# A second level of Strassen's scheme for one product in four pairs of column groups, in a fused encoder block on one core

## The chip, the core and the metric

The kernel runs on one core of a Trainium2 chip. It has TensorE (PE, matrix products; weight loads are shown as PEld), VectorE (DVE), ScalarE (ACT), GpSimd (POOL) and SyncE (SP, whose queue issues the transfers). The metric is the device time of one execution in microseconds (us); lower is better. Work is in float32 split into two float16 parts (a high part and what is left, the low part), so one product of two matrices is three matrix products: high × high, high × low, low × high (`PASSES`).

## The reference

One encoder layer over 1024 tokens of width 1024:

```python
u = rms_norm(x, norm1_g)
q, k, v, cb, cc, ch, ga, gb = jnp.split(u @ w_in, split_pts, axis=-1)
q, k = rms_norm(q, q_norm_g), rms_norm(k, k_norm_g)        # 8 heads of 64
y_a = neighbourhood_attention(q, k, v, rpb) @ w_attn_branch
y_b = short_gated_conv(cb, cc, ch, conv_w) @ w_conv_branch
merged = jax.nn.sigmoid(ga) * y_a + jax.nn.sigmoid(gb) * y_b
x = x + merged @ w_o
h = rms_norm(x, norm2_g) @ w_mlp_in                        # 1024 -> 4096
x = x + jnp.square(jax.nn.relu(h)) @ w_mlp_out             # 4096 -> 1024
```

## The kernel before

The stages follow each other on TensorE: V, Q and K with attention and convolution, the gates (eight blocks `n` of channels), the product with `w_o`, the first MLP product (`w_mlp_in`), the second (`w_mlp_out`). The change lies in the gates, in the first MLP product and in the way from it to the second.

**First MLP product.** The 4096 columns are done in 16 groups `q` of 256 columns. Each group is one level of Strassen's scheme in Winograd's form: the weights of the group and the activations are cut into 2 × 2 quarters, and `seven` does seven products (numbers 1 to 7) of the quarters' sums in place of eight. A product is a `unit` of twelve matmuls of 512 tokens (four slices of the inner dimension times three passes) into one of eight PSUM banks, which `anybank` hands out in turn. Groups 0 and 1 run in two halves of 256 tokens, groups 2 to 15 whole (`quad`). VectorE and ScalarE put the seven results together in the tile `as` (`z[0]` to `z[6]`): ScalarE copies product 1 into `z[4]`, VectorE adds product 6 (`z[5]`), and so on (`post6`, `post5`, `post7`, `post3`). Then `h_done` applies ReLU and Square on ScalarE, GpSimd adds the sums that the second product will need, and SyncE stores the tile in `HS`.

Ahead of it, `prep1` and `sums1` get the weights of a group ready: SyncE loads two raw tiles of 512 KB, ScalarE multiplies by `norm2_g` (`rows_scaled`), GpSimd adds the four sums of quarters (`tsum`), ScalarE takes Squares of the raw tiles for a scale (`forms_sum`), a matmul with a column of ones adds these over the partitions (L201, `all_sum`), VectorE makes the scale from it in six short instructions (`scale_of`), and ScalarE and VectorE write the high and the low parts (`forms_split`, L1184, L1188). The parts `w16_1` of consecutive groups lie in three buffers in turn (`TAGS`), so that group `q`'s may be written when group `q - 3` is done (`gate`).

**Second MLP product.** 28 steps `ops[16]` to `ops[43]`, each a product of high and low parts made from `h` (loaded back from `HS`) and from sums of the `w_mlp_out` tiles (`raw`, `w2x`). `prep2` gets the scale of a quarter of these weights (L1751, L1754, L1139, the ones matmul, L204) and then the parts: ScalarE the high parts (L1786, L1791), VectorE the low parts (L1788, L1797). A step waits in the program for the buffers of three steps before.

**What sets the order.** The order is made when the program is built: each `unit` on TensorE advances generators in the background (`tick` for `bg`, which gets weights ready; `step` for `fg`, which finishes results) by so many steps, and each step appends its instructions to its engine's queue. The engines then run their queues in that order. SyncE's queue is one as well: a load that waits for a free raw tile holds back all behind it. `load_upto` appends loads as raw tiles are said to be done.

Of the kernel before, what the change touches and what calls it, by code (L numbers as in the profile page):

```python
# [10 lines left out]
F32 = mybir.dt.float32  # L11
# [41 lines left out]
def encoder_block(ctx: ExitStack, tc: tile.TileContext, x, weights, cols, gqk, rel, masks, out):  # L53
# [24 lines left out]

    sc = base.tile([128, 540], F32, name="sc")
    sci = sc.bitcast(I32)  # L80
    area = {"keep": [0, 0, 172], "prep": [172, 172, 268], "tmp": [268, 268, 540]}

# [14 lines left out]
    def at(c, i, n=1):  # L97
        return slice(c.start + i, c.start + i + n)
# [79 lines left out]

    late, units, forced, side = [], [0], [False], [False]
    work = [0]  # L180
# [5 lines left out]
    def built(*chs):  # L186
# [5 lines left out]
        forced[0] = False  # L192
    ones, turn = base.tile([128, 132], BF16, name="ones"), [0]
    V.memset(ones, 1.0)
# [11 lines left out]

    def unit(mms, post=None, steps=0, ticks=0):

        for ps, l, r, a, b in mms:
            T.matmul(ps, l, r, start=a, stop=b)  # L210
# [126 lines left out]
    consts = keep(28)  # L337
    g1, g2, gm2 = at(consts, 0, 8), at(consts, 20, 8), keep()
    rows = {"A": lambda j: rowsA, "B": lambda j: rowsB, "O": lambda j: rowsM}
    chunks, offset = {}, 0  # L340
    for (kind, j), pieces in plan():
        ch = chunks[kind, j] = Chunk(kind, [(nk, sum(n for _, n in cs)) for _, _, nk, cs in pieces],
                                     {"A": "wa", "B": "wb"}.get(kind, "ws"), rows.get(kind, lambda j: g1)(j),
                                     j if kind == "V" else None, 9 if kind in "VQKCGS" else 0)
        ch.first = len(loads)
        for p, (k, w) in enumerate(ch.widths):
            ch.offs.append(offset)
            if kind != "X" and (kind, j) != ("1", 0) and (kind, j, p) != ("1", 1, 1):
                loads.append((ch, p))
            offset += 128 * k * w  # L350
    cG, cS = chunks["G", 0], {n: chunks["S", n] for n in range(1, 8)}
    cV, cConv, cA, cB, cO, c1, c2, c2x = ([chunks[k, j] for j in range(n)] for k, n in
# [888 lines left out]
    def gate_units(n, tail=None):  # L1241
# [32 lines left out]
        return sg  # L1274

    def branch_units(n, post):
        j, cc = n // 2, (n % 2) * 128
        for g, act, ch in ((0, actA, cA[j]), (1, actB, cB[j])):
            built(ch)
            for half in range(2):  # L1280
                ps = anybank()
                unit(ch_mms(ps, act, half, ch, 4, 256, cc),
                     lambda ps=ps, g=g, half=half, ch=ch: post(g, half, ps, sc[:, ch.inv]), 2, 4)

    for n in range(8):
# [5 lines left out]
        if n < 7:  # L1291
            sg = gate_units(n)
            if n in (1, 3, 5):
                push(cA[n // 2 + 1], cB[n // 2 + 1])
# [147 lines left out]
    def sums1(q):  # L1442

        ch = c1[q]
        if q == 2:
            yield from rows_scaled(ch, g2)
        if q == 0:
            tsum[0] = U2[1][:, 2].rearrange("p s k t -> p (s k t)").bitcast(F32).rearrange("p (i c) -> p i c", i=4)
        elif q % 2 == 0:
            t = wsp.tile([128, 2, 4, 512], F32, name="tsum", tag="ws")  # L1450
            for i in range(2):
                tsum[q + i] = t[:, i]
        if q != 2:
            yield from rows_scaled(ch, g2)
        yield from forms_sum(ch, tsum[q], 3 if q else 0)

    def prep1(q):

        ch = c1[q]
        s, ch.inv = yield from scale_of(ch.sum, 9, 1)  # L1460
        yield from gate(q)
        pool, tag = TAGS[q % 3]
        P = P1[q] = pool.tile([128, 7 if q else 8, 2, 512], F16, name="w16_1", tag=tag)
        yield from forms_split(ch, tsum[q], s, P)
        ready.add(q)
        if 1 < q < 15:
            yield from sums1(q + 1)

# [94 lines left out]

    bg.extend([first1(), prep_m()])
    side[0] = True
# [48 lines left out]
    def last_pair():  # L1614
# [24 lines left out]
    def h_done(q, c0=0, c1=512, wait1=0, wait2=0):  # L1639
# [26 lines left out]
    def quad(q, c0=0, c1=512):  # L1666
# [24 lines left out]
        def post3(ps):  # L1691
# [8 lines left out]
            2: lambda ps: V.tensor_tensor(z[0], ps[2], z[4], op=OP.add),  # L1700
            7: post7, 3: post3}, 2 if c1 == 512 else 3, 5, (1, 2, 5, 4, 6, 7, 3) if c0 else (1, 6, 5, 4, 2, 7, 3))

    def whole(q):
        quad(q)
        pe_done[0] = q + 1

    quad(0, 0, 256)
# [7 lines left out]
    held[0] = 0  # L1715
    for q in range(2, 14):
        whole(q)


# [16 lines left out]
    def prep2(s):  # L1736
# [26 lines left out]
        if s == 0:  # L1763
# [201 lines left out]
```

## Time and profile before

| | us |
|---|---|
| three runs | 1199.51, 1201.03, 1201.32 |
| median | 1201.03 |
| the profiled execution | 1199.51 |
| its span on the core | 1197.7 |
| TensorE busy | 1188.3 (99%) |
| VectorE busy | 939.3 (78%) |
| ScalarE busy | 753.0 (63%) |
| GpSimd busy | 432.9 (36%) |

The granted clock of TensorE is 1.00 in the whole run. In the span, the gates run from about 298 to 530 us, `w_o` to about 612, the first MLP product to 903.7 (groups 0 and 1 in halves to 649.5, then 18.15 us for each group; group 14 starts at 867.40 and group 15 at 885.53), and the second from there to 1191, in steps of 10.36 us. A row of a timeline gives the start, the length, the engine, the line, the instruction with what it writes and reads, and in brackets the idle time before it with what ended that.

### The profile page before, as it was taken

To read this page: it belongs to the slowest core of one execution; us is meant where nothing else is said; L and a number is where in the kernel's file an instruction comes from. 1 tells how busy PE (TensorE), PEld (TensorE's weight loads), DVE (VectorE), ACT (ScalarE), POOL (GpSimd) and SP (SyncE) were. 2 spreads that over 40 slices of the span, in tenths; PEclk is the share of its full clock that TensorE was granted. 3 is DMA by queue.
4 is the path that set the end of the run, shared out by engine and by line. 5 is a ranking of instruction groups with operands and counts; after the bars stand their busy time and mean duration, and the time that the engine had idled before them with its cause. 6 is when DMAs were issued, how large, how long until landed. Compare 5 with 4: busy or idle time off the path is not lost.

```text
span 1197.7 us, 16871 instructions
## 1 busy us (share of the span) xinstructions
PE 1188.3 (99%) x6206; PEld 573.6 (48%) x6206; DVE 939.3 (78%) x1708; ACT 753.0 (63%) x1169; POOL 432.9 (36%) x292
## 2 busy tenths in 40 slices
PE   8999999999999999999999999999999999999998
PEld 6444445555444444444467444444444444444444
DVE  6799898898478786878888745645649999999997
ACT  7866578776554554336779768778576743746440
POOL 2640012222320312001014466565577471554662
PEclk9999999999999999999999999999999999999999
DMA  9949557666452121233386545535465926335302
GB/s 288 220 158 205 114 128 138 116 141 138 104 130 68 38 71 36 71 139 142 74 161 197 177 149 177 170 127 187 159 237 202 376 80 233 112 140 194 106 36 106
DMA packets 177250, 174.91 MB, mean 146 GB/s; under 512 B 137744, under 2 KB 138256, under 8 KB 173072
## 3 DMA queue, kind: packets, MB, share of 16 engines
q1 hardware_dynamic: 177168, 173.84, 49.6%
q8 instruction: 48, 0.79, 0.3%
q14 instruction: 34, 0.28, 0.1%
HBM read 102.51 MB, written 37.75 MB: 117 GB/s over the span
## 4 chain that ended last, share of the span: by engine, by line
PE 79%; DVE 13%; ACT 5%; issue 2%; DMA 0%; POOL 0%; DVEq 0%; ACTq 0%
PE ps_d L210 27%; PE ps_s L210 24%; PE ps_o L210 17%; PE ps_d L1060 8%; DVE w_s L1184 2%; PE ps_s L980 1%; PE ps_o L1037 1%; DVE s L498 1%; DVE sg L1300 1%; ACT w_ws L266 1%; DVE w_ws L297 1%; DVE q L764 1%; DVE qs L751 1%; ACT sq L439 1%; ACT w_ws L306 1%
## 5 line engine op out<-in xcount | busy, mean ns | idle before, releaser
L210 PEld LDWEIGHTS <-ops 128*128 128x128 f16 x1356 | 132.5, 98 | 157.3
L210 PEld LDWEIGHTS <-w 128*128 128x128 f16 x1368 | 132.8, 98 | 139.5
L1060 PE MATMUL ps_d<-uT,w_ws 128*128 128x512 f16 x528 | 123.7, 379 | 0.0
L210 PE MATMUL ps_d<-ops 128*128 128x512 f16 (+1 forms) x528 | 118.3, 374 | 0.0
L1786 ACT ACTIVATE ops<-hf,sc 128x2048 f16<-128x2048 f32 x26 | 52.0, 2000 | 97.7 <-PE ps_o L210 35.2
L210 PE MATMUL ps_s<-ops 128*128 128x512 f16 x492 | 112.9, 379 | 0.0
L1173 POOL TENSOR_TENSOR tsum<-raw 128x512 f32<-128x512 f32 x28 | 46.2, 1665 | 148.9 <-ACT raw L1159 148.7
L1366 POOL TENSOR_TENSOR as<-as 128x512 f32<-128x512 f32 x56 | 77.5, 1385 | 38.4 <-ACT as L1646 35.1
L210 PEld LDWEIGHTS <-w_s 128*128 128x128 f16 x588 | 56.8, 98 | 69.6 <-DVE w_s L1184 2.1
L210 PEld LDWEIGHTS <-uT 128*128 128x128 f16 x528 | 51.4, 98 | 62.1 <-DMA uT<-u 0.2
L210 PE MATMUL ps_d<-u2x,w 128*128 128x512 f16 (+1 forms) x360 | 80.0, 372 | 0.0
L1788 DVE SCALAR_TENSOR_TENSOR ops<-hf,sc,ops 128x2048 f16<-128x2048 f32 x26 | 74.0, 2846 | 4.6 <-ACT ops L1786 4.6
L1060 PEld LDWEIGHTS <-w_ws 128*128 128x128 f16 x528 | 51.3, 98 | 54.1
L210 PE MATMUL ps_o<-ops 128*128 128x512 f16 x336 | 77.1, 379 | 0.0
L210 PE MATMUL ps_o<-u2T,w 128*128 128x512 f16 (+1 forms) x324 | 71.7, 371 | 0.0
L1159 ACT ACTIVATE raw<-raw,sc 128x256 f32<-128x256 f32 x172 | 71.0, 494 | 0.1
L1173 POOL TENSOR_TENSOR gsum<-raw 128x512 f32<-128x512 f32 x14 | 19.0, 1379 | 132.9 <-ACT raw L1159 59.9
L1188 ACT ACTIVATE w<-raw,sc 128x512 f16<-128x512 f32 (+1 forms) x28 | 24.6, 927 | 54.1 <-DVE sc L432 54.1
L1679 DVE TENSOR_TENSOR as<-ps_d,as 128x512 f32<-128x512 f32 (+1 forms) x14 | 9.4, 672 | 55.8 <-ACT as L1698 53.4
L210 PE MATMUL ps_s<-u2T,w 128*128 128x512 f16 (+1 forms) x252 | 52.7, 359 | 0.0
L1003 ACT ACTIVATE sz<-sz,sc 128x384 f32<-128x384 f32 (+1 forms) x64 | 37.3, 582 | 23.9 <-DVE sc L994 16.6
L306 ACT ACTIVATE w_ws<-raw,sc 128x512 f16<-128x512 f32 (+2 forms) x72 | 40.6, 637 | 17.6 <-DVE sc L279 17.6
(374 smaller groups left out, 2621.5 us busy)
## 6 DMA issues: line engine op xcount, KB each, us to landing
raw<-in_weights SPq DMA_DIRECT2D x88, 512.0 KB, 5.3
hs<-as SPq DMA_DIRECT2D x16, 1792.0 KB, 8.8
hf<-hs SPq DMA_DIRECT2D x26, 1024.0 KB, 7.1
w2x<-in_weights SPq DMA_DIRECT2D x16, 512.0 KB, 8.5
raw<-in_weights SPq DMA_DIRECT2D x16, 384.0 KB, 3.8
xt<-in_x SPq DMA_DIRECT2D x8, 512.0 KB, 8.2
gs<-s SPq DMA_DIRECT2D x4, 1024.0 KB, 3.9
x<-in_x SPq DMA_DIRECT2D x8, 512.0 KB, 9.8
```

The source lines that it names most:

```text
L210: T.matmul(ps, l, r, start=a, stop=b)
L266: A.activation(self.parts[:, 1, :k * w].bitcast(BF16), self.raw[p][:, :k * w], AF.Square, accum_out=sc[:, at(rm, p)])
L306: A.activation(self.parts[:, 0, f + o:f + o + m], self.raw[p][:, o:o + m], AF.Copy, scale=sc[:, c:c + 1])
L1003: A.activation(z, z, AF.Exp, scale=-1.0, bias=sc[:, d["mx"]], accum_out=sc[:, d["sm"]])
L1060: T.matmul(ps, l, r, start=a, stop=b)
L1159: A.activation(v, v, AF.Copy, scale=sc[:, at(g, 4 * i + k)])
L1173: G.tensor_tensor(t[:, o], a, b, op=OP.add)
L1184: V.scalar_tensor_tensor(o(1), w, sc[:, s], o(0), op0=OP.mult, op1=OP.subtract)
L1188: A.activation(o(0), w, AF.Copy, scale=sc[:, s])
L1366: sub.tensor_tensor(z[o], z[a], z[b], op=op)
L1786: A.activation(P[:, 1, 0], hf, AF.Copy, scale=sc[:, Rs])
L1788: V.scalar_tensor_tensor(P[:, 1, 1], hf, sc[:, Rs], P[:, 1, 0], op0=OP.mult, op1=OP.subtract)
```

## The change

1. *Second level.* For the pairs of groups (6, 7), (8, 9), (10, 11) and (12, 13), product 1 of both groups of a pair (24 matmuls of 512 tokens) is done as one: the left quarter of both groups, side by side, is cut in 2 × 2 again, and seven products of six matmuls of 256 tokens each give the two results (`slices`). They are summed in three PSUM banks, in three units of 18, 12 and 12 matmuls (`THREE`) with one ordinary product between two of them. ScalarE and VectorE read the banks between the units (`p0`, `p1`, `p2`). The sums of quarters of the activations are made once (`quarters`, in groups 2 and 3), those of the weights for each pair (`deep1`).
2. *Norms early.* The Squares that give the scales of groups 2 to 15 are taken in the gates (`norms1`): the weights are loaded there once more, 28 loads of 512 KB, into three rooms that turn free, and `scales1` makes all scales with one matmul of ones of seven columns.
3. *Buffers and order.* The parts `w16_1` lie in two buffers ("V" and "B"), since the parts of the slices take the third, and are written when group `q - 2` is done. Each background generator prepares a pair (`prep_pair`). The store of a group's result comes four steps later in the program (`wait(4)`), groups 3 to 13 advance the background by two ticks a product, and the matmul of ones of the second MLP product's first scale stands one unit later (`scale_of(sums, 0, 4)`).

The core of the diff:

```diff
-    def unit(mms, post=None, steps=0, ticks=0):
+    def unit(mms, post=None, steps=0, ticks=0, free=False):
         for ps, l, r, a, b in mms:
-            T.matmul(ps, l, r, start=a, stop=b)
+            T.matmul(ps, l, r, start=a, stop=b, skip_group_check=free)
+        for g in list(hooks):
+            if not advance(g):
+                hooks.remove(g)
...
+    def norms1(t, first):
+        for _ in range(first):
+            yield
+        for q in range(2, 16):
+            for i in range(2):
+                if (2 * q + i) % 3 == first:
+                    SP.dma_start(t, bass.AP(tensor=weights.tensor, ...))
+                    for _ in range(4):
+                        yield
+                    A.activation(t, t, AF.Square, accum_out=sc[:, at(sum1, 2 * (q - 2) + i)])
+                    yield
...
     def prep1(q):
-        pool, tag = TAGS[q % 3]
-        P = P1[q] = pool.tile([128, 7 if q else 8, 2, 512], F16, name="w16_1", tag=tag)
+        P = P1[q] = base2.tile([128, 8, 2, 512], F16, name="w16_1", tag="B")
...
+    def main1(q):
...
+        while pe_done[0] < q - 1:
+            yield
+        m = int(deep)
+        pool, tag = ((base, "V"), (base2, "B"))[q % 2]
+        P = pool.tile([128, 7 - m, 2, 512], F16, name="w16_1", tag=tag)
...
+        yield from parts([...], at(s1, q // 2 - 1), then)
+        ready.add(q)
...
+    def deep1(q):
+        x, y = c1[q].r[0], c1[q + 1].r[0]
+        d = sub["t"][:, 1, 0:2].rearrange("p a (h c) -> p (a h) c", h=2)
+        b11, b21, b12, b22 = x[:, 0, :256], x[:, 0, 256:], y[:, 0, :256], y[:, 0, 256:]
+        for o, a, b in ((0, b11, b12), (1, b12, b22), (2, d[:, 0], b22), (3, d[:, 2], b21)):
+            V.tensor_tensor(d[:, o], a, b, op=OP.add)
...
-        bg.append(sums1(2))
-        bg.extend(prep1(q) for q in range(2, 16))
+        sub["t"] = wsp.tile([128, 2, 4, 512], F32, name="tsum", tag="ws")
+        bg.append(prep_pair(2))
...
+        yield from wait(4 if q > 1 else 0)
         SP.dma_start(HS[q // 4][:, :, q % 4], f)
...
+        def p0():
+            A.activation(y, b("a"), AF.Copy)
+            add(zb[:, lo], b("b"), y)
+        def p1():
+            add(zb[:, hi], b("b"), y)
+            less(zb[:, hi], b("c"), zb[:, hi])
+        def p2():
+            A.activation(za[:, lo], b("a"), AF.Copy)
+            add(za[:, hi], b("b"), y)
+            less(zb[:, lo], b("c"), zb[:, lo])
+            ends()
...
+        first = slices(q, 0, z[4], zp, sub["y"], ends)
+        advance(first)
+        need(q)
+        main(q, ps, 5, None)
+        advance(first)
+        main(q, ps, 6, None)
+        advance(first)
+        for i, post in ((2, p2), (4, None), (7, p7), (3, p3)):
+            main(q, ps, i, post, ticks)
...
-    for q in range(2, 14):
+    bg.extend(prep_pair(q) for q in range(4, 16, 2))
+    for q in range(2, 6):
         whole(q)
+    need("quarters")
+    for q in range(6, 14, 2):
+        pair(q)
...
-        sw, inv = yield from scale_of(sums, 0)
+        sw, inv = yield from scale_of(sums, 0, 4)
```

**VectorE, at the end of group 14 and in group 15.** `as_8334` (before) and `as_8364` (after) are group 15's result tile; `h0` and `raw` feed the first low parts, of `ops[16]` (`ops_8263`, `ops_8307`). Before (L1692 is the last post of group 14, L204 to L433 make the scale, L1679 is group 15's first post, L1788 and L1797 write low parts):

```order
L1692 TENSOR_TENSOR as_8207<-ps_d_8318,as_8207 128x512
L204 TENSOR_SCALAR sc_71<-ps_o_8352 128x1
L426 TENSOR_SCALAR sc_71<-sc_71 128x1
L428 TENSOR_SCALAR sc_71<-sc_71 128x1
L430 TENSOR_SCALAR sc_71<-sc_71 128x1
L432 TENSOR_SCALAR sc_71<-sc_71 128x1
L433 TENSOR_SCALAR sc_71<-sc_71 128x1
L1679 TENSOR_TENSOR as_8334<-ps_d_8355,as_8334 128x512
L102 TENSOR_TENSOR sc_71<-sc_71 128x1
L1788 SCALAR_TENSOR_TENSOR ops_8263<-h0_8223,sc_71,ops_8263 128x2048
L1797 SCALAR_TENSOR_TENSOR ops_8263<-raw_7891,sc_71,ops_8263 128x1024
L1797 SCALAR_TENSOR_TENSOR ops_8263<-raw_8039,sc_71,ops_8263 128x1024
```

In the changed kernel L1829 is the last post of group 14, L1816 group 15's first, L204 to L442 make the scale, L2036 and L2045 write low parts:

```order
L1829 TENSOR_TENSOR as_8224<-ps_o_8348,as_8224 128x512
L1816 TENSOR_TENSOR as_8364<-ps_s_8383,as_8364 128x512
L204 TENSOR_SCALAR sc_71<-ps_o_8398 128x1
L435 TENSOR_SCALAR sc_71<-sc_71 128x1
L437 TENSOR_SCALAR sc_71<-sc_71 128x1
L439 TENSOR_SCALAR sc_71<-sc_71 128x1
L441 TENSOR_SCALAR sc_71<-sc_71 128x1
L442 TENSOR_SCALAR sc_71<-sc_71 128x1
L1821 TENSOR_TENSOR as_8364<-ps_d_8401,as_8364 128x512
L102 TENSOR_TENSOR sc_71<-sc_71 128x1
L2036 SCALAR_TENSOR_TENSOR ops_8307<-h0_8269,sc_71,ops_8307 128x2048
L2045 SCALAR_TENSOR_TENSOR ops_8307<-raw_7978,sc_71,ops_8307 128x1024
```

Group 15's first post now stands ahead of the six scale rows, and its second (L1821) ahead of the product of the scales (L102); before, the second came behind the low parts of `ops[16]`.

**SyncE, around the start of group 14.** `hs3` is the store of a result tile (group 12's first, group 13's later), `raw` and `w2x` are loads of weights, `h0` and `ops` loads of stored results. Before:

```order
L1657 DMA hs3_5334<-as_7928 896x1x512
L234 DMA raw_8183<-in_weights 128x1024
L234 DMA raw_8185<-in_weights 128x1024
L234 DMA w2x_8224<-in_weights 128x1024 x4
L1824 DMA h0_8223<-hs0_5331 128x2048
L1657 DMA hs3_5334<-as_8077 896x1x512
L1767 DMA ops_8350<-hs0_5331 128x2048
```

In the changed kernel:

```order
L1794 DMA hs3_5391<-as_7931 896x1x512
L237 DMA raw_8246<-in_weights 128x1024
L237 DMA raw_8248<-in_weights 128x1024
L237 DMA w2x_8270<-in_weights 128x1024 x4
L2072 DMA h0_8269<-hs0_5388 128x2048
L1794 DMA hs3_5391<-as_8106 896x1x512
L2015 DMA ops_8380<-hs0_5388 128x2048
```

The order of the rows is the same; the two raw loads wait for other tiles, those of group 15's weights, whose parts are now written after group 13 is done.

**ScalarE, in one group before and around one slice unit now.** Before, the scaling of raw tiles (L1159), two Squares for the norm (L1168), Relu and Square of the group before (L1644, L1646), the copy of product 1 (L1698), then high parts (L1188):

```order
L1159 ACTIVATE raw_7458<-raw_7458,sc_71 128x2x128 x4
L1159 ACTIVATE raw_7600<-raw_7600,sc_71 128x2x128 x4
L1168 ACTIVATE tsum_7624,sc_71<-raw_7458 128x1024
L1168 ACTIVATE tsum_7624,sc_71<-raw_7600 128x1024
L1644 ACTIVATE as_7639<-as_7639 128x2048
L1646 ACTIVATE as_7639,sc_71<-as_7639,sc_71 128x2048
L1698 ACTIVATE as_7783<-ps_o_7784 128x512
L1188 ACTIVATE w16_1_7884<-raw_7458,sc_71 128x512
L1188 ACTIVATE w16_1_7884<-raw_7600,sc_71 128x2x512
L1188 ACTIVATE w16_1_7884<-tsum_7624,sc_71 128x2x512 x2
L1159 ACTIVATE raw_7602<-raw_7602,sc_71 128x2x128 x4
L1159 ACTIVATE raw_7745<-raw_7745,sc_71 128x2x128 x4
```

In the changed kernel L1511 scales raw tiles, L1866 is the copy in `p0` and L1874 that in `p2` (both read the bank `ps_o_7932`), L1780 and L1782 are Relu and Square, L1197 writes high parts:

```order
L1197 ACTIVATE w16_1_7838<-raw_7680,sc_71 128x2x512
L1197 ACTIVATE w16_1_7838<-tsum_6097,sc_71 128x2x512 x2
L1511 ACTIVATE raw_7682<-raw_7682,sc_71 128x2x128 x4
L1866 ACTIVATE zt4_7042<-ps_o_7932 128x256
L1780 ACTIVATE as_7817<-as_7817 128x2048
L1197 ACTIVATE w16_1_7970<-raw_7682,sc_71 128x2x512
L1782 ACTIVATE as_7817,sc_71<-as_7817,sc_71 128x2048
L1197 ACTIVATE w16_1_7970<-tsum_6097,sc_71 128x2x512 x2
L1874 ACTIVATE as_7931<-ps_o_7932 128x256
L1511 ACTIVATE raw_7684<-raw_7684,sc_71 128x2x128 x4
L1511 ACTIVATE raw_7856<-raw_7856,sc_71 128x2x128 x4
L1780 ACTIVATE as_7931<-as_7931 128x2048
```

The two Squares for the norm are gone, and the copies after the slice units stand each in a place of its own between the other rows.

More of the change, by code (lines that the diff above doesn't have):

```diff
@@ L177, in flush @@
         forced[0] = False
-    late, units, forced, side = [], [0], [False], [False]
+    late, units, forced, side, hooks = [], [0], [False], [False], []
     work = [0]
@@ new lines, in quarters, with pace @@
+    def quarters():
+        def pace():
+            yield from apart(units[0], 1)
+        sub["a"] = wsp.tile([128, 4, 2, 2, 256], F16, name="a16_d", tag="ws")
+        f = base.tile([128, 7, 512], F32, name="quarter", tag="K")
+        u = u2T[:, 0]
+        for t in range(2):
+            hi, lo = (u[:, i, :, 256 * t:256 * t + 256] for i in range(2))
+            V.tensor_tensor(f[:, 2 * t:2 * t + 2].rearrange("p h (k c) -> p (h k) c", k=2), hi, lo, op=OP.add)
+            yield from pace()
+        yield from sums(f, V)
+        for a, b, v in ((0, 1, f[:, 2:3]), (1, 4, f[:, 4:7])):
+            hi, lo = (sub["a"][:, a:b, i].rearrange("p f k c -> p f (k c)") for i in range(2))
+            A.activation(hi, v, AF.Copy)
+            yield from pace()
+            V.tensor_tensor(lo, v, hi, op=OP.subtract)
+            yield from pace()
+        ready.add("quarters")
```

183 lines of the change are left out of this document (162 added, 21 removed).

## The prediction

> **What bounds the kernel now.** I read the page first. Its busy line and the line of the chain that ended last, by engine:
>
> ```profile
> PE 1188.3 (99%) x6206; PEld 573.6 (48%) x6206; DVE 939.3 (78%) x1708; ACT 753.0 (63%) x1169; POOL 432.9 (36%) x292
> ...
> PE 79%; DVE 13%; ACT 5%; issue 2%; DMA 0%; POOL 0%; DVEq 0%; ACTq 0%
> ```
>
> TensorE is busy for 1188.3 of 1197.7 us. The chain's 13% of VectorE only says whose result TensorE took up last. Whether TensorE stands still is seen in its waits (line, what released it, us in total, times, longest):
>
> ```profile
> PE ps_o L565 <- DMA xt<-in_x: 4.6, 1, 4.6
> PE ps_s L980 <- DVE sc L994: 0.5, 1, 0.5
> PE ps_s L210 <- DVE w_s L1184: 0.3, 1, 0.3
> PE ps_d L210 <- DVE w_s L1184: 0.2, 1, 0.2
> ```
>
> That is the first load of x and three waits of half a microsecond or less. So a shorter matmul stream shortens the run one for one, while every other engine may take more work until it makes TensorE wait. Next I read TensorE's timeline in the first MLP product (start, length, instruction, count):
>
> ```profile
> 631.18 1.47 PE L210 MATMUL ps_d<-u2T,w 128*128 128x256 f16 x12
> 632.49 1.47 PE L210 MATMUL ps_s<-u2T,w 128*128 128x256 f16 x12
> ...
> 649.54 2.75 PE L210 MATMUL ps_o<-u2T,w 128*128 128x512 f16 x12
> 652.13 2.75 PE L210 MATMUL ps_d<-u2x,w 128*128 128x512 f16 x12
> ...
> 659.90 0.17 PE L201 MATMUL ps_s<-ones 128*128 128x1 bf16 x1
> 659.93 1.24 PE L210 MATMUL ps_o<-u2T,w 128*128 128x512 f16 x5
> ```
>
> Starts give the stream: twelve matmuls of 256 columns take 632.49 − 631.18 = 1.31 us (109.2 ns each), twelve of 512 take 2.59 us (215.8 ns each), and a one-column matmul of L201 pushes the next by 659.93 − 659.90 = 0.03 us. Last, the other engines' load in two stretches, gates and MLP (span, then length, busy us and count for PE, weight loads, DVE, ACT, POOL; clock, DMA share, GB/s):
>
> ```profile
> 380.00:400.00 20.00, 19.88 (x93) 8.89 (x92) 14.79 (x26) 11.53 (x19) 5.46 (x4) 1.00 0.18 54
> 700.00:750.00 50.00, 50.00 (x235) 22.65 (x234) 27.56 (x50) 38.31 (x58) 30.85 (x23) 1.00 0.50 167
> ```
>
> ScalarE is busy for 11.53 of 20 us in the gates and 38.31 of 50 in the MLP, VectorE 14.79 of 20 and 27.56 of 50. There is room, if the new work falls into the gaps.
>
> **What the change takes from TensorE.** In four pairs, product one of both groups is 2 × 12 matmuls of 512, 24 × 215.8 ns = 5.18 us, and becomes seven slices of six matmuls of 256, 42 × 109.2 ns = 4.59 us. That is 0.59 us a pair, 2.37 us for four. Fourteen one-column matmuls become one: 13 × 0.03 = 0.39 us. Sum: −2.76 us. It counts in full, since nothing else holds TensorE there.
>
> A rule of the Trainium skill speaks against this. "TensorE: Matmul & The Clock Gate", section Back-to-back issue gap, calls N/2.4 + 2.5 ns the gap of an isolated matmul, and gives a sustained spacing of about 81 ns for 128 columns and 131 ns for 512. An estimate on a line between these is 98 ns for 256, by which a pair would lose 42 × 98 − 24 × 131 = 0.97 us, the change 3.9. The rows above, with a weight load for every matmul, don't agree: 215.8 ns and 109.2 ns are what that page gives for the isolated one.
>
> **Norms in the gates.** 28 loads of 512 KB and 28 Squares over 1024 columns come in. The price of a Square is L1168's (gate stage, busy, mean ns):
>
> ```profile
> L1168 ACT ACTIVATE gsum<-raw 128x1024 f32<-128x1024 f32 x14 | 14.8, 1054 | 0.3
> ```
>
> With its read of the accumulator, some 0.2 us, 28 × 1.25 = 35 us of ScalarE over about 190 us that have 8.5 us in 20 free. SP is handed 28 more issues; each waits for the Square that last read its room, and raw loads queue behind. But a load has four TensorE units (10.4 us) ahead of its Square, and at 54 GB/s, a DMA share of 0.18, it has the engines nearly for itself. At most two or three Squares in a row (3.8 us) stand ahead of the splits of the next gate's weights. I take nothing, with 0 to 2 us as its bounds: the low end because TensorE had no wait to lose there, the high end if half of such a burst hits once. In exchange MLP groups 2 to 15 lose 28 Squares and their VectorE scalars: no TensorE time.
>
> **Support for the slices.** Per pair four deep sums and seven 256-wide posts on VectorE, the weight parts of the slices, two 256-wide copies on ScalarE. Prices of the kinds (busy, mean ns):
>
> ```profile
> L1184 DVE SCALAR_TENSOR_TENSOR w<-raw,sc,w 128x1024 f16<-128x1024 f32 x12 | 15.3, 1279 | 0.3 <-ACT w L1188 0.3
> ...
> L1366 DVE TENSOR_TENSOR as<-as 128x256 f32<-128x256 f32 x8 | 3.4, 423 | 0.2
> ```
>
> Eleven × 0.42 = 4.6 us and about 3 us of low parts, less the posts and low parts of two products of 512 which go: some 4 us per pair of 36 us, where VectorE has 16 us free (27.56 of 50). The once-only quarter sums (24 × 256 columns, under 24 × 0.42 = 10 us) push the posts of group 2 back. Weights are ready groups ahead. Nothing, unless slices wait on ScalarE (second rival).
>
> **The way into the second MLP product.** Two buffers for split weights in place of three put the splits of group 15 behind the end of group 13; raw loads freed by them stand ahead of the w2x loads in SP's queue. I count from the first matmul of group 14, t = 0. ops[16] is the second MLP product's first:
>
> ```profile
> 867.40 2.75 PE L210 MATMUL ps_o<-u2T,w 128*128 128x512 f16 x12
> ...
> 903.69 2.75 PE L210 MATMUL ps_s<-ops 128*128 128x512 f16 x12
> ```
>
> ops[16] starts at t = 36.3, ops[17] 4 × 2.59 later at 46.65. What leads there now: SP's issues and the landing of w2x (median us),
>
> ```profile
> 863.80 1.62 SPq L234 DMA_DIRECT2D raw<-in_weights  x2
> 865.48 2.85 SPq L234 DMA_DIRECT2D w2x<-in_weights  x4
> 868.42 0.42 SPq L1824 DMA_DIRECT2D h<-hs  x1
> ```
>
> ```profile
> w2x<-in_weights SPq DMA_DIRECT2D x4, 512.0 KB, 9.2
> ```
>
> then ScalarE (squares L1751, L1754; Relu, Square and z copy of group 14/15; high parts of ops[16]),
>
> ```profile
> 874.34 1.14 ACT L1751 ACTIVATE ops<-raw,sc 128x1024 bf16<-128x1024 f32 x1
> ...
> 879.42 2.00 ACT L1754 ACTIVATE ops<-w2x,sc 128x2048 bf16<-128x2048 f32 x1
> ...
> 881.55 2.00 ACT L1754 ACTIVATE ops<-w2x,sc 128x2048 bf16<-128x2048 f32 x1
> ...
> 887.17 1.91 ACT L1644 ACTIVATE as<-as 128x2048 f32<-128x2048 f32 x1 [3.53 <-DVE as L1692]
> 889.12 2.00 ACT L1646 ACTIVATE as<-as,sc 128x2048 f32<-128x2048 f32 x1
> ...
> 891.12 0.58 ACT L1698 ACTIVATE as<-ps_s 128x512 f32<-128x512 f32 x1
> 891.60 1.99 ACT L1786 ACTIVATE ops<-h,sc 128x2048 f16<-128x2048 f32 x1
> ```
>
> and VectorE:
>
> ```profile
> 883.67 0.16 DVE L1139 TENSOR_REDUCE sc<-sc 128x1 f32<-128x6 f32 x1 [7.61 <-ACT ops L1754]
> ...
> 888.36 0.16 DVE L204 TENSOR_SCALAR sc<-ps_o 128x1 f32<-128x1 f32 x1 [1.22 <-PE ps_o L201]
> ...
> 889.18 0.14 DVE L433 TENSOR_SCALAR sc<-sc 128x1 int32<-128x1 int32 x1
> 891.73 0.69 DVE L1679 TENSOR_TENSOR as<-ps_d,as 128x512 f32<-128x512 f32 x1 [2.40 <-ACT as L1698]
> ...
> 893.62 2.44 DVE L1788 SCALAR_TENSOR_TENSOR ops<-h,sc,ops 128x2048 f16<-128x2048 f32 x1 [1.04 <-ACT ops L1786]
> 895.99 4.50 DVE L1797 SCALAR_TENSOR_TENSOR ops<-raw,sc,ops 128x1024 f16<-128x1024 f32 x2
> ...
> 901.01 3.84 DVE L1788 SCALAR_TENSOR_TENSOR ops<-ops,sc 128x2048 f16<-128x2048 f32 x1
> ...
> 907.89 5.89 DVE L1797 SCALAR_TENSOR_TENSOR ops<-h,sc,ops 128x1024 f16<-128x1024 f32 x2
> 913.71 2.34 DVE L1788 SCALAR_TENSOR_TENSOR ops<-hf,sc,ops 128x2048 f16<-128x2048 f32 x1
> ```
>
> Before: w2x issued at −1.9, its squares end at 16.2, the sum of the norms (L1139) stands at 16.3, the scale is there at 21.9 (889.18 + 0.14), low parts start at 26.2 and ops[17] is ready at 46.4 (907.89 + 5.89). The second half of its first product starts 1.3 us after 46.65 and takes its first low part one matmul later, 48.15: 1.8 us to spare.
>
> After: the last post of group 13 ends at 0.9. ScalarE then has Relu 1.9, a high part of 512 (0.7, from the 1024 below), Square 2.0 and a high part of 1024 ahead; a low part on VectorE frees the raw tile:
>
> ```profile
> L1188 ACT ACTIVATE w<-raw,sc 128x1024 f16<-128x1024 f32 x11 | 12.5, 1133 | 0.0
> ```
>
> That makes 0.9 + 1.9 + 0.7 + 2.0 + 1.1 + 1.3 (the 1279 ns above) = 7.9. The raw load goes, and 0.8 later (two took 1.62) w2x, from 8.7 to 10.8 for the last: 10.6 us later than now. ScalarE, at 6.6 after that high part, has two more (2.3), a z copy (0.6) and the four L1751 squares (874.34 to 879.42, 5.1) before it needs w2x at 14.6, and would end at 18.8 (4.2 for L1754) if the loads were there; with 9.2 us of landing the last is there at 20.0, and the squares end at 22.2. I take 20.4, by the middle. So the norms' sum comes 4.1 later.
>
> The five posts of group 14 behind it on VectorE end at 23.9 (883.67 to 887.17 is 3.5 us); Relu, Square and the z copy of group 15 follow (887.17 to 891.73: 4.56), and the order now has the post on that copy (z5) ahead of the six scale rows, where before the scale went first. So z5 at 28.5, scale at 29.1 + 0.96 = 30.1, high part 1.99, low parts from 32.1: 5.9 later than 26.2. The other post (0.6 us, 900.41 to 901.01) now lies under the high part, so ops[17] is ready at 46.4 + 5.9 − 0.6 = 51.7. With 0.1 us for the signal TensorE has waited 51.8 − 48.15 = 3.65, say **3.7 us**, of it about 1 at ops[16]. With the ends 18.8 and 22.2 it is 2.1 and 5.5. Later products are covered: at 913.71 VectorE was to wait 2.48 us for ScalarE before ops[18], and this idle time goes first.
>
> **Sum.** The profiled execution took 1199.51 us, 1.81 more than its span. 1199.51 − 2.76 + 3.7 = 1200.45. It is the fastest of three runs (1199.51, 1201.03, 1201.32), 1.52 under the median; on the median's footing 1202.0. A measurement can tell 0.2% from no change, 2.4 us: from 1198.6 to 1203.4 is "the same". The forecast's own range is 1200.4 to 1203.8.
>
> **Rivals.**
> - *Clean gain.* The w2x loads land soon and the copy of group 15 slips ahead, or TensorE needs the low parts later than I think; then only −2.76 is left: 1201.03 − 2.76 = 1198.3. For it: the margin of 1.8 us takes part of the delay, and the chain has eight links, each of which I may have too late. Against: each link is in the order of the program. 0.24.
> - *Slices wait (slower).* The second slice unit adds into the banks of the first, so ScalarE's copy and VectorE's add of it must be done within the one product between them, 2.59 us; copy, add and signals are about 1.0, so 1.6 is to spare. If ScalarE stands in a Relu and a Square (1.9 + 2.0 = 3.9 us) as the slice ends, TensorE waits up to 2.3 us, say 1.25, once per pair: 4 × 1.25 = 5.0 us, without or with the 3.7: 1203.3 to 1207.0. It decides from a copy that starts 1.6 us after its slice. Against: the copy stands ahead of the Relu of the group before. 0.20.
> - *Matmul pace (slower).* If matmuls of 256 with three banks open take over 5.18 us / 42 = 123 ns, product one gains nothing; halfway between 109.2 and 215.8, at 162.5 ns, a pair loses 1.65 us: 1201.03 + 6.6 − 0.39 + 3.7 = 1210.9. Against: the 109.2, measured with a weight load for every matmul. 0.03. By the figures of the Trainium skill's page on TensorE (above) alone, the time would be 1201.03 + 3.9 = 1204.9.
> - *A longer wait on the way in.* The forecast's upper end, over 5.1 us: 1203.4 to 1203.8. 0.10.
>
> **Numbers.** Forecast without change 0.43. Faster 0.24, the same 0.43, slower 0.20 + 0.03 + 0.10 = 0.33. The range goes from the clean gain, 1198.3 less 0.5 for spread of runs, to the slices' 1207.0 less 0.5, since its upper end needs both waits: 1197.8 to 1206.5; left out is the matmul pace and the ends of the others.
>
> **What would show it.** Slices: twelve 256-wide matmuls in 1.31 us, three units of 18, 12 and 12. Gates: no TensorE wait over 0.5 us. Group 14 to ops[17]: w2x issued 8 to 9 us after the group's start, L1139's row 20 us after, TensorE idle for about 1 us at ops[16] and 2.7 at ops[17], released by VectorE's low parts (L1797). Wrong if TensorE doesn't wait there, or waits inside the pairs.

## The result and the profile after

The changed kernel takes 1204.39 us (median of 9 runs, 1203.29 to 1205.79) against 1200.11 us for the kernel before (9 runs, 1199.07 to 1201.38): the ratio is 1.0034, interval 1.0024 to 1.0045, so 4.3 us slower. The time lies in the range given, but not where the forecast put it (the same); it is on the side of the slower rivals. The profiled execution took 1205.79 us, the slowest of the nine, with a span of 1204.0. Its busy line and the line of the chain:

```profile
PE 1186.2 (99%) x6265; PEld 579.7 (48%) x6265; DVE 975.0 (81%) x1654; ACT 754.7 (63%) x1175; POOL 455.3 (38%) x292
...
PE 61%; DVE 23%; ACT 8%; issue 5%; DMA 2%; SPq 0%; DVEq 0%; POOL 0%; ACTq 0%
```

TensorE has 2.1 us less to do and yet the span is 6.3 us longer; in the chain VectorE's share went from 13% to 23%. The waits of TensorE (line, releaser, total us, times, longest) say where:

```profile
PE ps_o L574 <- DMA xt<-in_x: 4.5, 1, 4.5
PE ps_s L210 <- DVE ops L2045: 2.6, 2, 1.8
PE ps_s L210 <- DVE w_s L1193: 1.1, 1, 1.1
PE ps_d L210 <- DVE w L1193: 1.1, 1, 1.1
PE ps_d L210 <- DVE as L1824: 0.9, 1, 0.9
PE ps_d L546 <- DVE ones L609: 0.7, 1, 0.7
PE ps_o L210 <- DVE x L2144: 0.7, 1, 0.7
PE ps_d L210 <- DVE ops L2045: 0.7, 1, 0.7
PE ps_s L989 <- DVE sc L1003: 0.5, 1, 0.5
PE ps_d L210 <- DVE w_s L1193: 0.2, 1, 0.2
```

Three lines stood there before: the first load, L989's 0.5 and the 0.2 of w_s. New are 3.3 us at the operands of the second MLP product (L2045), 1.1 us at group 4's weights (L1193 w), 0.9 us at a bank (as L1824), 0.7 us near the end (x L2144); the gates' wait went from 0.3 to 1.1 us, and one of 0.7 us in the first 10 us changes from profile to profile (0 to 1.8). The slices run as fast as forecast: in TensorE's timeline six matmuls start every 0.655 us, 109 ns each.

```profile
724.22 0.82 PE L210 MATMUL ps_d<-u2T,w_d 128*128 128x256 f16 x6
724.88 0.82 PE L210 MATMUL ps_s<-a_d,w_d 128*128 128x256 f16 x6
725.53 0.82 PE L210 MATMUL ps_o<-a_d,w_d 128*128 128x256 f16 x6
```

What is lost is seen when TensorE's starts in the changed kernel are set against those before, place by place:

| place | before, us | after, us | after − before |
|---|---|---|---|
| first attention product | 147.46 | 147.47 | 0.01 |
| `w_o` | 529.86 | 530.79 | 0.93 |
| group 2 | 649.54 | 650.45 | 0.91 |
| ops[16] | 903.69 | 904.29 | 0.60 |
| last unit | 1191.25 | 1196.43 | 5.18 |

A listed wait costs 0.16 us more than it lists, since a matmul is shown for 379 ns and starts every 216. With that, gates 0.85; groups 2 to 15: −2.76 + 1.08 + 0.89 + 2 × 0.16 = −0.47 (the table has −0.31); second MLP product: 3.25 + 0.69 + 4 × 0.16 = 4.58 (the table has 4.58). The sum is 5.0 of 5.2 us. The other 1.1 of the 6.3 us of span lie behind TensorE's work: from the last unit's start to the landing of the last store both kernels take 5.5 us, and then the program's closing semaphore instructions take 0.91 us before and 2.05 after. With one profile of the kernel before, it is not shown whether that belongs to the change.

The way into the second MLP product, after: TensorE (start of group 14, which is t = 0, and of ops[16]), SyncE, ScalarE, VectorE.

```profile
868.00 2.75 PE L210 MATMUL ps_s<-u2T,w 128*128 128x512 f16 x12
...
904.29 1.67 PE L210 MATMUL ps_d<-ops 128*128 128x512 f16 x7
```

```profile
872.31 4.26 SPq L237 DMA_DIRECT2D raw<-in_weights  x2
876.63 1.94 SPq L237 DMA_DIRECT2D w2x<-in_weights  x4
```

```profile
884.16 2.00 ACT L2002 ACTIVATE ops<-w2x,sc 128x2048 bf16<-128x2048 f32 x1 [2.18 <-DMA w2x<-in_weights]
...
887.49 2.00 ACT L2002 ACTIVATE ops<-w2x,sc 128x2048 bf16<-128x2048 f32 x1 [1.23 <-DMA w2x<-in_weights]
...
897.53 1.99 ACT L2034 ACTIVATE ops<-h,sc 128x2048 f16<-128x2048 f32 x1
```

```profile
889.61 0.16 DVE L1148 TENSOR_REDUCE sc<-sc 128x1 f32<-128x6 f32 x1 [7.93 <-ACT ops L2002]
...
897.66 0.69 DVE L1816 TENSOR_TENSOR as<-ps_s,as 128x512 f32<-128x512 f32 x1 [4.58 <-ACT as L1835]
898.27 0.15 DVE L204 TENSOR_SCALAR sc<-ps_o 128x1 f32<-128x1 f32 x1
...
899.81 2.35 DVE L2036 SCALAR_TENSOR_TENSOR ops<-h,sc,ops 128x2048 f16<-128x2048 f32 x1
...
913.97 5.87 DVE L2045 SCALAR_TENSOR_TENSOR ops<-h,sc,ops 128x1024 f16<-128x1024 f32 x2
```

w2x is issued at t = 8.6 (forecast 8.7), ScalarE's squares wait 2.18 and 1.23 us for it, the norms' sum stands at 21.6 (20.4), group 15's first post at 29.7 (28.5), the low parts begin at 31.8 (32.1), and ops[17] is ready at 51.8 (51.7).

### The profile page after: what moved, and what is told of

It is laid out like the page before. It is cut to its first block, busy times and chain, and to the rows that moved or that the text cites. A ratio compares the mean times of both kernels' runs of the same rounds, so it can differ in the third digit from the quotient of the medians.

```text
span 1204.0 us, 16986 instructions
## 1 busy us (share of the span) xinstructions
PE 1186.2 (99%) x6265; PEld 579.7 (48%) x6265; DVE 975.0 (81%) x1654; ACT 754.7 (63%) x1175; POOL 455.3 (38%) x292
## 4 chain that ended last, share of the span: by engine, by line
PE 61%; DVE 23%; ACT 8%; issue 5%; DMA 2%; SPq 0%; DVEq 0%; POOL 0%; ACTq 0%
PE ps_s L210 19%; PE ps_d L210 18%; PE ps_o L210 13%; PE ps_d L1069 8%; DVE ops L2045 2%; DVE ops L2036 2%; DVE w_s L1193 2%; PE ps_s L989 1%; PE ps_o L1046 1%; DVE w L1193 1%; DVE s L507 1%; ACT as L1782 1%; DMA w2x<-in_weights 1%; DVE sg L1342 1%; DVE w_ws L300 1%
## 5 line engine op out<-in xcount | busy, mean ns | idle before, releaser
L210 PEld LDWEIGHTS <-w 128*128 128x128 f16 x1272 | 124.3, 98 | 129.3 <-DVE w L1193 1.6
L1408 POOL TENSOR_TENSOR as<-as 128x512 f32<-128x512 f32 x56 | 104.1, 1858 | 47.4 <-ACT as L1782 44.1
L210 PE MATMUL ps_d<-ops 128*128 128x512 f16 x516 | 118.4, 379 | 0.7 <-DVE ops L2045 0.7
L1520 POOL TENSOR_TENSOR tsum<-raw 128x512 f32<-128x512 f32 x28 | 39.4, 1417 | 126.9 <-ACT raw L1511 126.9
L210 PE MATMUL ps_o<-ops 128*128 128x512 f16 (+1 forms) x348 | 77.1, 372 | 0.7 <-DVE x L2144 0.7
L2036 DVE SCALAR_TENSOR_TENSOR ops<-hf,sc,ops 128x2048 f16<-128x2048 f32 x26 | 74.0, 2847 | 2.3 <-ACT ops L2034 2.2
L210 PE MATMUL ps_d<-u2T,w 128*128 128x512 f16 (+1 forms) x288 | 60.9, 361 | 0.9 <-DVE as L1824 0.9
L1193 DVE SCALAR_TENSOR_TENSOR w<-raw,sc,w 128x1024 f16<-128x1024 f32 (+1 forms) x20 | 24.2, 1220 | 44.0 <-ACT w L1197 44.0
L1780 ACT ACTIVATE as<-as 128x2048 f32<-128x2048 f32 (+1 forms) x18 | 30.9, 1718 | 42.3 <-DVE as L1857 25.7
L1193 DVE SCALAR_TENSOR_TENSOR w<-tsum,sc,w 128x1024 f16<-128x1024 f32 x28 | 50.7, 1834 | 5.1 <-ACT w L1197 5.1
L210 PE MATMUL ps_s<-u2x,w 128*128 128x512 f16 (+1 forms) x228 | 49.8, 368 | 0.0
```

Source lines behind the costliest of these rows:

```text
L210: T.matmul(ps, l, r, start=a, stop=b, skip_group_check=free)
L1193: V.scalar_tensor_tensor(o(1), w, sc[:, s], o(0), op0=OP.mult, op1=OP.subtract)
L1408: sub.tensor_tensor(z[o], z[a], z[b], op=op)
L1520: G.tensor_tensor(t[:, o], a, b, op=OP.add)
L1780: A.activation(v[:, 0:4], v[:, 0:4], AF.Relu)
L2036: V.scalar_tensor_tensor(P[:, 1, 1], hf, sc[:, Rs], P[:, 1, 0], op0=OP.mult, op1=OP.subtract)
```

## The experiments

Times are medians; "over before" is against the kernel before on the same chip. The changed kernel itself, run again, was 4.3 us over (e5). "e" numbers name the runs.

**e1: the scale ahead again.**

```diff
-        sw, inv = yield from scale_of(sums, 0, 4)
+        sw, inv = yield from scale_of(sums, 0)
```

> Only the matmul of ones for the second MLP product's first scale is put back by one unit, so the six scale rows stand ahead of group 15's first post on VectorE, as in the kernel before. The prediction's chain says that the swapped order holds the low parts back by about 1.7 us (scale 1.0, post 0.7): by it the TensorE wait at ops[16] and ops[17] falls from 3.25 us to about 1.6 and the time by 1.7 us. The rival, from the trace of the changed kernel: ScalarE's high part of ops[16] (897.53 to 899.52) ends last whatever the order, the low part began at 899.81; then the low parts gain 0.3 us at most, TensorE waits 1.3 us at the matmul of ones (it would stand at 888.72, its column is ready at 889.97) and as much less at ops[16] and ops[17], and the time stays within 0.5 us of the changed kernel's.

Measured: 1203.50 us, 3.96 over before, ratio 1.0035 (1.0022 to 1.0047). In VectorE's timeline the first low part now waits for ScalarE's high part:

```profile
898.96 2.35 DVE L2036 SCALAR_TENSOR_TENSOR ops<-h,sc,ops 128x2048 f16<-128x2048 f32 x1 [1.13 <-ACT ops L2034]
```

The order gives the low parts next to nothing, as the rival said (the 1.3 us wait at the matmul of ones that it foretold is not there); the shorter wait in this profile (1.83 us at ops[17]) came from w2x, for which ScalarE waited 1.7 us in place of 3.4. Unexpected was that the 0.7 us wait near the end is gone. It is there in all five profiles with `scale_of(sums, 0, 4)` (after, e2 to e5: 0.68 to 0.70 us) and in none of the seven without. The argument holds for all four quarters of the second MLP product, and VectorE's low parts in the last one come 1.75 us later against TensorE's end: the last of them starts 14.76 us before TensorE's last matmul in e1, 13.01 us before it in e2.

**e2: w2x early.** The tile for `h0` is taken and the four loads are issued before group 14, ahead of the raw loads that wait for group 15's splits.

```diff
+    later["h0"] = wsp.tile([128, 2, 4, 512], F32, name="h0", tag="ws")
+    w2x_load(0)
     bg.append(first2())
```

> Only the four w2x loads are issued ahead of the two raw loads that wait for group 15's splits. If those loads are the head of the chain into the second MLP product, they are issued by 870 us in place of 876.6, the squares of w2x follow the squares of raw without a gap and end at about 886.2 in place of 889.6, all behind it comes 3.4 us earlier, the TensorE wait at ops[16] and ops[17] falls from 3.25 us to under 0.5, and the time falls by about 3.2 us. If the wait comes from elsewhere (the splits themselves, GpSimd beside VectorE), the squares end earlier and the wait stays over 2 us.

SyncE and VectorE:

```profile
866.57 4.25 SPq L237 DMA_DIRECT2D w2x<-in_weights  x4
```

```profile
886.52 0.16 DVE L1148 TENSOR_REDUCE sc<-sc 128x1 f32<-128x6 f32 x1 [4.82 <-ACT ops L2002]
...
896.73 2.35 DVE L2036 SCALAR_TENSOR_TENSOR ops<-h,sc,ops 128x2048 f16<-128x2048 f32 x1
```

In the profile the mechanism is as expected: issue of w2x at 866.57, the norms' sum 3.1 us earlier (886.52 against 889.61), the low parts too, and of 3.25 us of wait 0.48 is left. The last unit starts 2.9 us earlier (1193.52 against 1196.43). But the median is 1203.69 us, 4.15 over before, ratio 1.0033 (1.0020 to 1.0045), and the profiled run (1202.80) is among the fastest. The expected fall of 3.2 us would leave 1.1 over before; the interval, 2.4 to 5.4 us, excludes that. So the wait is shown to go, and its full worth in time is not. Part of the gap is that the wait varies with the landing of w2x (3.25 us in the first profile, of the slowest of nine runs, 2.59 in e5, 1.83 in e1, 0.92 in e3), so the median of the changed kernel may hold less of it; that, and what else there is, is not shown.

**e3: no norms in the gates.**

```diff
-                hooks.extend(norms1(t, i) for i, t in enumerate(rooms))
+                V.memset(sc[:, sum1], 1024.0)
```

> The 28 loads and Squares for the norms in the gates are left out; the sums they would give are set to a constant, so the scales of groups 2 to 15 are not those of the weights. If they cost only through the one longer wait in the gates (1.14 us at 448 us against 0.29 before), that wait falls to 0.3 and the time falls by 0.9 us. If 35 us of ScalarE and 14 MB of loads cost more than that, beside other work, the time falls by 2 us or more.

Measured: 1201.73 us, 2.19 over before, ratio 1.0018 (1.0009 to 1.0027), 2.1 less than the changed kernel. The wait at w_s is back to 0.2 us:

```profile
PE ps_s L210 <- DVE w_s L1193: 0.2, 1, 0.2
```

So 0.9 us is shown. The other 1.2 us is not in the gates: in this profile w2x landed sooner (0.92 us of wait at ops[17]). Whether the norms have to do with that is not shown.

**e4: no slices.** The loads are in the old order, too.

```diff
-    DEEP = range(6, 14)
+    DEEP = range(0)
...
-        pair(q)
+        whole(q)
+        whole(q + 1)
```

> The second level is taken out: groups 6 to 13 do product one as 12 matmuls of 512 each; all else of the change (two buffers, norms early, quarter sums of the activations, now unused) stays. By the matmul sum TensorE's stream is 2.4 us longer; the 0.89 us wait at 727 us goes: the time rises by 1.5 us. The rival: the slices' work on VectorE (13 us more in 700 to 750 us than before) and the GpSimd sums beside it (1.83 us for one in place of 1.32) cost more than the slices save; then the time falls.

Measured: 1204.95 us, 5.41 over before, ratio 1.0049 (1.0035 to 1.0062): 1.1 us more than e5, with intervals that overlap. TensorE's starts say more. The 0.9 us wait at the bank is gone, and from group 2 to ops[16] TensorE takes 1.04 us longer than in the kernel before, where e5 takes 0.49 less. So the slices save 1.5 us there as the kernel stands, 2.4 without that wait. The rival, that their work on VectorE and GpSimd costs more than they save, fell.

**e5: the control.**

> The changed kernel as it is, once more, on the same chip as the next three. Its time should be 4.3 us over the kernel before (ratio 1.0034); its TensorE waits at 448, 691, 727 us and at the end should stand at 1.1, 1.1 to 1.3, 0.9 and 0.7 us as before, and those at ops[16] and ops[17] move with the landing of the w2x loads, between 1 and 3.3 us.

1204.14 us, 4.30 over before, ratio 1.0035 (1.0023 to 1.0048). Waits at 448, 691 and 727 us and near the end: 1.14, 0.91, 0.89 and 0.68 us; at ops[17] 0.75 + 1.84.

**e6: e1 and e2 together.**

> The scale put ahead again (first experiment) and the w2x loads issued early (second). Theory: the second experiment kept a late matmul of ones in every quarter of the second MLP product, which left VectorE 1.7 us late in the last quarter and cost 0.7 us of TensorE at 1186 us; the first kept the late loads, 1.8 us at ops[17]. Together neither is left: no TensorE wait over 0.3 us after 727 us, last matmuls start at 2.3 - 0.5 - 0.7 = 1.1 us after those of the kernel before, and the time is 2 us under the control. The rival, that these waits are covered by something that profiles don't show (single experiments brought no measurable time): within 0.7 us of the control.

1201.99 us, 2.15 over before, ratio 1.0018 (1.0009 to 1.0027), 2.15 under the control: as expected. It is more than the 0.3 and 0.2 us of e1 and e2 together; each of those rests on five runs, and why they gave so little is not shown. At ops[17] 0.33 us is left, near the end nothing. (The last matmuls start 2.47 us later than before, 1.67 of that from the first 10 us.)

**e7: the quarter sums earlier.** On e6:

```diff
-        if q == 4:
-            yield from quarters()
...
             yield from main1(n)
+            if n == 2:
+                while pair_done[0] < 4:
+                    yield
+                yield from quarters()
```

> As the one before, and the quarter sums of the activations stand in the second halves of groups 0 and 1, before the parts of group 3, and not after them. If these sums hold back group 1's store and by that group 3's copy, ScalarE's high parts and group 4's parts, the 1.1 to 1.3 us wait at 691 us goes and the time falls by 1.1 us against the one before. If group 4's parts are late for another reason (GpSimd beside VectorE, the raw loads) the wait stays.

1208.28 us, 6.3 more than e6: the wait at group 4 grew to 2.8 us and more came behind it. Some 1.5 us of it is no wait: in this profile the granted clock of TensorE is 0.50 from 693.8 us, in the second of two waits at group 4, to 697.2, and the ten matmuls from 694.17 on take 3.65 us in place of 2.16. The reason for the waits is the chain that the wait hangs on. In the changed kernel SyncE stores group 1's result late, ScalarE's copy into the tile that this frees (group 3's) waits for it, and Relu, Square and the high parts of group 4 stand behind that copy; VectorE's low parts last ran beside GpSimd's sums (3.91 us for two). The store before, then the store, the copy and the low parts after:

```profile
662.12 0.53 SPq L1657 DMA_DIRECT2D hs<-as  x1
```

```profile
671.30 0.53 SPq L1794 DMA_DIRECT2D hs<-as  x1
```

```profile
677.85 0.60 ACT L1835 ACTIVATE as<-ps_d 128x512 f32<-128x512 f32 x1 [4.24 <-DMA hs<-as]
```

```profile
687.01 3.91 DVE L1193 SCALAR_TENSOR_TENSOR w<-tsum,sc,w 128x1024 f16<-128x1024 f32 x2
```

In e7 the sums of group 1 were pushed back further, the store went later and the copy waited for 13.7 us:

```profile
677.09 0.53 SPq L1797 DMA_DIRECT2D hs<-as  x1
```

```profile
686.27 0.60 ACT L1838 ACTIVATE as<-ps_d 128x512 f32<-128x512 f32 x1 [13.71 <-DMA hs<-as]
```

So the edit pushed the store the other way, and that shows the chain: a store at 662.1 us with no wait (before), at 671.3 with 1.1, at 677.1 with 2.8.

**e8: the norms' cycle.** On e6, in `norms1`:

```diff
-                    for _ in range(4):
+                    for _ in range(3):
```

> As e6_both, but each Square for the norms in the gates comes one TensorE unit earlier after its load (a cycle of 4 units and not 5). The work on ScalarE and the loads are the same. If the wait at 448 us comes from the place of two Squares (they push GpSimd's sums under VectorE's adds of m at 420 us, 1.75 and 0.98 us in place of 0.80 and 0.69), it goes back to 0.3 us or another appears at another gate; if it comes from the amount of ScalarE work, it stays at 1.1 us.

1205.38 us, 3.4 more than e6: four waits (0.18 to 1.38 us, 2.9 in all, against 1.14 in e6) between 444 and 451 us. Behind them the granted clock falls. TensorE's timeline, then two rows of its clock (window, length, busy us and count, clock, DMA share, GB/s):

```profile
450.80 3.86 PE L210 MATMUL ps_s<-qD,w_s 128*128 128x512 f16 x10 [1.38 <-DVE w_s L1193]
454.45 2.96 PE L210 MATMUL ps_d<-uT,w_s 128*128 128x512 f16 x12
```

```profile
452.00:453.00 1.00, 1.00 (x4) 0.50 0.93 373
453.00:454.00 1.00, 1.00 (x3) 0.50 0.20 82
```

Ten matmuls take 3.65 us in place of 2.16. So the same work in other places costs 1.8 us more of waits and 1.5 us of clock. In the eleven profiles other than those of e7 and e8, the clock is 1.00 from the first 10 us to the end of TensorE's work. Two of the four waits, of 0.34 and 1.04 us, are for ScalarE's high parts, and their way was not followed. What a place does is seen before the 448 us wait of the changed kernel. VectorE's adds of m, before and after:

```profile
420.29 0.80 DVE L1302 TENSOR_TENSOR m<-sg 128x512 f32<-128x512 f32 x1
...
421.79 0.69 DVE L1302 TENSOR_TENSOR m<-sg 128x512 f32<-128x512 f32 x1
```

```profile
419.99 1.75 DVE L1344 TENSOR_TENSOR m<-sg 128x512 f32<-128x512 f32 x1
...
422.43 0.98 DVE L1344 TENSOR_TENSOR m<-sg 128x512 f32<-128x512 f32 x1
```

and GpSimd's sums, before and after:

```profile
417.93 2.61 POOL L1173 TENSOR_TENSOR gsum<-gsum,raw 128x512 f32<-128x512 f32 x2 [0.81 <-ACT gsum L1168]
```

```profile
419.91 2.95 POOL L1182 TENSOR_TENSOR gsum<-gsum,raw 128x512 f32<-128x512 f32 x2 [1.02 <-ACT gsum L1177]
```

Two Squares ahead of ScalarE's scaling put GpSimd's second pair of sums from 417.93 to 419.91, under the adds, which take 1.75 and 0.98 us in place of 0.80 and 0.69. VectorE is 0.93 us late from there on and TensorE waits 0.85 us more. "SBUF — State Buffer" of the Trainium skill, section SBUF: two separate sides, says that a VectorE instruction with two inputs from SBUF and a GpSimd instruction that reads SBUF exclude each other on a shared pair of ports, for a whole instruction; these rows agree, with an add of 1.75 us beside the sums.

**e9: the store earlier.** On e6, in `quad`:

```diff
-...((16, 16), (2, 5))...
+...((16, 10), (2, 1))...
```

> e6_both, and the last half of group 1's sums stands ahead of the quarter sums on VectorE (it is appended after 10 and 1 steps in place of 16 and 5), so group 1's result is stored earlier. The earlier runs give the store's issue and the wait at 691 us: 662.1 and none (kernel before), 671.3 and 1.1 (changed kernel), 677.1 and 2.8 (e7). If the store sets that wait (ScalarE's copy of group 3 waits for the tile that it frees), the store is issued by 668 us, the wait is under 0.3 us and the time falls by 0.9 us against e6. If the quarter sums' length alone does it, the wait stays at 0.9.

1199.96 us, ratio 0.9997 (0.9989 to 1.0006): against the kernel before, 2.2 us better than e6. The store and the copy:

```profile
668.53 0.53 SPq L1794 DMA_DIRECT2D hs<-as  x1
```

```profile
676.45 0.57 ACT L1835 ACTIVATE as<-ps_d 128x512 f32<-128x512 f32 x1
```

The copy waits for nothing, and both the wait at 691 us and the one at 727 us are gone. That is more than expected: the second goes with the same lateness. In the changed kernel the engines hand it on: ScalarE's Relu waits 3.19 us (at 715.02) for VectorE's last post of the group before, and VectorE's low parts wait 3.02 us (at 718.01) for ScalarE's high parts; in e9 the same rows stand 0.92 us earlier, though its TensorE started 1.2 us later.

**e10: one tick in group 5.** On e9:

```diff
-...2 if 2 < q < 14 else 5...
+...(1 if q == 5 else 2) if 2 < q < 14 else 5...
```

> e9, and in group 5 the background is advanced by one tick a product in place of two, so the parts of group 6 stand later on VectorE's queue against the posts of group 5. If the 0.9 us wait at 727 us (a slice unit's bank, released by a post, L1824) comes from these parts standing ahead of the posts, it goes and the time falls by 0.9 us; the price could be late parts of group 6 (a wait released by L1193 in the first pair). If the wait is set by GpSimd's sums beside VectorE, it stays.

1199.92 us, ratio 0.9996 (0.9987 to 1.0005): nothing against e9, where that wait was gone already. The order did change; VectorE in e9 and in e10 (the post L1816 behind the parts, then ahead of them):

```profile
721.63 2.04 DVE L1193 SCALAR_TENSOR_TENSOR w<-tsum,sc,w 128x1024 f16<-128x1024 f32 x1 [0.16 <-ACT w L1197]
723.60 0.68 DVE L1816 TENSOR_TENSOR as<-ps_o,as 128x512 f32<-128x512 f32 x1
```

```profile
718.40 0.69 DVE L1816 TENSOR_TENSOR as<-ps_o,as 128x512 f32<-128x512 f32 x1 [1.18 <-ACT as L1835]
719.44 2.23 DVE L1193 SCALAR_TENSOR_TENSOR w<-tsum,sc,w 128x1024 f16<-128x1024 f32 x1 [0.35 <-ACT w L1197]
```

**e11: another phase of the norms.** On e10, in `norms1`:

```diff
-        for _ in range(first):
+        for _ in range((0, 1, 3)[first]):
```

> e10, and the loads and Squares of the norms start at units 0, 1, 3 in place of 0, 1, 2; their number and their cycle stay. If the place of single Squares sets the longer wait in the gates, the wait at 448 us (1.14 us in all runs with norms but e8) changes, down to 0.3 or up as in e8; if the amount of work on ScalarE sets it, it stays at 1.14. The version that takes all of the waits away would stand at 0.998 of the kernel before.

1198.62 us, ratio 0.9987 (0.9978 to 0.9995), 1.4 us under the kernel before. All waits of TensorE over 0.4 us:

```profile
PE ps_o L574 <- DMA xt<-in_x: 4.3, 1, 4.3
PE ps_s L210 <- DVE w_s L1193: 0.5, 1, 0.5
PE ps_s L989 <- DVE sc L1003: 0.5, 1, 0.5
PE ps_d L546 <- DVE ones L609: 0.5, 1, 0.5
```

The wait in the gates went from 1.15 to 0.52 us with the same Squares. VectorE's second add of m:

```profile
421.62 1.60 DVE L1344 TENSOR_TENSOR m<-sg 128x512 f32<-128x512 f32 x1
```

Less the 0.52 us by which TensorE started late, it ends 0.22 us later than in the kernel before (0.93 in the changed kernel), and the wait is 0.23 us longer than there (0.85). The last unit starts at 1189.61, 1.64 us earlier than before, though the first 10 us took 0.5 longer: 2.16 of the 2.76 us.

## Why the prediction was right or wrong

- *TensorE's saving, −2.76 us.* Right. 109 ns a matmul; e11 has 2.16 us of it with 0.2 us of wait too many in the gates. The rival of the matmul pace, and with it the sustained figures of the Trainium skill's page "TensorE: Matmul & The Clock Gate" (section Back-to-back issue gap), fell for this stream: it starts a matmul every 109 and 216 ns.
- *The way into the second MLP product, +3.7 us.* Right in mechanism and place, and in this profile in size: 0.67 us at ops[16] and 2.58 at ops[17], 3.25 (forecast about 1 and 2.7), and 3.7 with the 0.16 that each wait costs besides. Other profiles with late w2x loads have 0.92 to 2.59. e2 and e6 take it away by its head, the w2x loads. One link was wrong and hid in the sum: I let ScalarE's high part of ops[16] wait for the scale. It runs at 897.53 with the scale at 899.2, so the order of the scale rows costs at most 0.3 us there (the high part ends at 899.52, the low part starts at 899.81), not 1.7; the squares came 1.2 us later than I took. The errors offset each other, so that the size came out so close is luck.
- *Where the sum failed: "I take nothing", three times.* Gates: 0.9 us, within the bounds of 0 to 2, by two Squares in a row, the point that I named and priced at nothing. Quarter sums: "push the posts of group 2 back"; I looked at posts and parts, not at the store of group 1, whose tile group 3's copy needs: 1.1 us. The first pair's bank: 0.9 us, near the second rival, but not it: the ordinary product between two slice units waits for the bank of group 5's post, by the lateness from the item before, once and not in each pair; the slice units and the later pairs didn't wait. Two of the signs that I named went against me by this: a wait over 0.5 us in the gates, and one inside a pair.
- *An edit seen at one of its places.* `scale_of(sums, 0, 4)` works in four quarters; I followed it in the first and missed 0.7 us near the end.
- *Cost on VectorE.* I took 4 us per pair of 36 us. In 700 to 750 us VectorE was busy 40.87 us against 27.56, 13 us in 50. About 6.7 us of that are rows that run longer than their kind elsewhere (low parts from sums of quarters 1.80 us and not 1.28, deep sums of two raw tiles 1.07 and not 0.42); the rest is new work, of two pairs in this window. GpSimd's sums of results went from 1.32 us to 1.83 (93.2 us for 51 against 68.8 for 52 between 600 and 900 us). My seven posts of 256 columns for a pair are five in the program. That this ate the margins is argued; no run tests it alone.
- *The sum.* Against the kernel before the forecast was −2.76 + 3.7 = +0.9 us and the measurement is +4.3, 3.4 more; the four terms that I had at nothing are 0.85, 1.1, 0.9 and 0.7 us, 3.5 together. That these agree to 0.1 is partly chance, since the terms are of the slowest execution, which has the longest wait at w2x and a longer end, and 4.3 is of the medians. So "the same", at 0.43 the likeliest case, was the wrong one: the steps had the sign of each term, but not the small ones.

Left open: why the program's end behind the last store's landing takes 0.91 us in the one profile of the kernel before and 1.2 to 2.05 in all others; what of e3's gain does not stand in the gates; and why e2's median fell so little.

## What to carry to other kernels

Where one engine has no stalls, a saving on it is worth what the others leave of it: go through every buffer that a moved piece of work delays, stores included, and ask who needs it next. A load's place in a queue is set by the one ahead of it that waits longest; issuing it earlier took away the largest wait of the first profile. Take the waits away together and measure the sum: two single edits were worth 0.3 and 0.2 us by the time of five runs each, and the two together 2.15. And look at the granted clock before a slower run is put down to its waits: in e7 and e8 some 1.5 us were clock.

## What was not expected of the hardware

The same 28 Squares in the gates cost TensorE 0.2, 0.85 or over 4 us, by their place alone (e11, e6, e8). In the first two it goes through GpSimd's sums that fall beside VectorE's adds of two inputs from SBUF: an add of 0.69 us took up to 1.75. In the third some 1.5 us of it is the granted clock, 0.50 for 3.41 us behind four waits of 2.9 us in 7; a single wait of 1.14 us, or the 0.74 and 1.84 us within 4 us at ops[17], was not followed by such a fall.
